# A hybrid Fourier and attention layer on one core: queues, engines and last rows changed, pl and the gate's sums in attention on GpSimd and ScalarE

## The chip, the cores and the metric

The kernel runs on one core of a Trainium2 chip. TensorE multiplies matrices into PSUM; VectorE (DVE), ScalarE (ACT) and GpSimd (POOL) work on tiles of 128 partitions; SyncE (SP) issues most DMAs, and ScalarE and GpSimd have DMA queues of their own. Each engine runs its own instructions in order. The metric is the device time of one execution in microseconds, as the median of several runs.

## The reference

One layer of a diffusion backbone over 1024 latent tokens (width 1024) with 256 context tokens, in float32. The cut below leaves out the rotary positions, the shapes and the context's own outputs.

```python
mod = silu(c) @ w_ada + b_ada
sh_m, sc_m, gt_m, sh_f, sc_f, gt_f = split(mod, 6)
h_lat = rms_norm(x, g_pre_mix) * (1 + sc_m) + sh_m
u_f, q_a, kv_a, kr = split(h_lat @ w_in)
q = rms_norm(q_a, g_q_a) @ w_q_b
k_nope, v = split(rms_norm(kv_a, g_kv_a) @ w_kv_b)
attn = softmax(q @ k.T * scale) @ v
four = fft2(u_f).real @ w_fourier
y = concat(four, attn) @ w_out
x = x + gt_m * rms_norm(y, g_post_mix)
h2 = rms_norm(x, g_pre_ffn) * (1 + sc_f) + sh_f
x = x + gt_f * rms_norm((silu(h2 @ w_gate) * (h2 @ w_up)) @ w_down, g_post_ffn)
```

There are 8 heads of 64 + 32 query columns, 1280 keys (latent and context), 4 Fourier groups of 128 channels, and 2816 hidden columns in the channel mixer.

## The kernel before, in words

**Products.** Every float32 product is made of three matmuls in a reduced format: a source is split into a high half, rounded by one engine (`split`, L50 on ScalarE), and a low half, the source minus the high half, made by VectorE (L56, written "v") or GpSimd (L58, written "p"). So each operand costs an operation on ScalarE and one on VectorE or GpSimd.

**Order.** The code is written as Python generators that interleave the work; a list scheduler turns it into one fixed instruction order for each engine and queue, starting from program order and from its own model of what is ready. Some instructions are pinned (`keep_in_program_order`), and `issue_after` puts a block behind one instruction of its engine. At run time each engine follows its order and waits on semaphores. A tile of a pool has `bufs` slots; a load into a slot waits until the slot's former readers are done.

**Stages.** (1) `constants` loads 83 rows of vectors, takes the Silu and transposes them. (2) `first_tiles` sweeps over j = 0 to 7: for each j it loads a block of w_ada (raw `araw`), splits it (ah, al), multiplies it with c (`modulation`: aps, then arow, cps, the shift SH and scale A), modulates a strip of x (h, L264), splits it (hh, hl), loads and splits a strip of w_in (`win_split`) and accumulates the projection of the first two token tiles. The modulation runs two steps ahead of the projection. `normed` (L198) loads a tile of x and normalises it. (3) `other_tiles` does the other eight token tiles, with `late_ada`, which sums w_ada's rows for two more modulations (`ada_sums`, L408), between them. (4) `fourier` does the DFT; in it `attention_weights` (L549) loads and splits the attention weights, and the keys, queries and maxima of head 0 are made. (5) `attention` (L584) goes over 8 heads and, in each, 10 blocks of 128 keys. For a block: scores S (6 matmuls), p32 = exp(S) on ScalarE, ph on ScalarE, pl on VectorE or GpSimd; two blocks later (LAG = 2) `pv` adds ph and pl times V into O. Between these steps `prepare` makes the next head's keys, queries (L686; the rotary part ends in the add of L701, then Qh on ScalarE and Ql on GpSimd) and `greatest` (L706), the maximum of each query's scores: 24 matmuls, each read by VectorE's reduction mx (L715). Their negatives become row 96 of Qh, by a DMA to DRAM from SP and one back from GpSimd. `finish` (L727) takes O and its sums through DRAM to get their reciprocals as rows, rb, and multiplies (L738). The gate gt_m is a sum of eight products of rows of w_ada with a column (`gate`, L441, `ada_sums`), one at blocks 3 and 8 of each head, by VectorE (L416, L418), behind its last split. (6) `output_weights` and `output_projection`. (7) `gate_up` and `down`, the channel mixer, with products cut down by Strassen-like sums; their operands are streamed through slots of `raw` and `unit`. (8) The end of `down`: the last products come in row tiles, the first halves of rows 0 to 3 (n = 2) and of rows 4 to 7 (n = 5), then the second halves of rows 0 to 3 (n = 3) and 4 to 7 (n = 4). For each row tile VectorE adds the bank to the accumulator (L1190), ScalarE takes the mean square, GpSimd the power -1/2 (L1212), VectorE scales by it and by the gate Gf (L1170), and GpSimd's DMA adds the row to `out` in DRAM. The last row tile is added to a copy of x1 loaded before, in two halves (L1175), and stored by SP and ScalarE.

Three spots of the code before:

```python
self.split(ph, pl, p32, "a", "v" if k % 3 == 1 or (h == HEADS - 1 and k % 2) else "p")
with tc.issue_after(self.lastv.ins):
    next(gate, None)
nc.sync.dma_start(self.max_d[h, :].rearrange("(b c) -> b c", b=NT), mrow)
nc.gpsimd.dma_start(Qh[96:97, :], self.max_d[h:h + 1, :])
```

Of the kernel before, what the change touches and what calls it, by code (L numbers as in the profile page):

```python
# [2 lines left out]

# [6 lines left out]
F32 = mybir.dt.float32  # L10
# [3 lines left out]
ALU = mybir.AluOpType  # L14
# [25 lines left out]
class Block:  # L40
# [49 lines left out]
    def build(self):  # L90
# [3 lines left out]
        with ExitStack() as top:  # L94
            self.cst = pool(top, "cst", side="left")
            self.dram = top.enter_context(tc.tile_pool(name="dram", bufs=1, space=DRAM))
            for name, n in (("xt", 7 * P), ("xtl", P), ("sum", HEADS), ("max", HEADS), ("inv", HEADS)):
                setattr(self, name + "_d", self.dram.tile([n, D], F32, name=name + "_d"))
# [68 lines left out]
    def constants(self):  # L167
        tc, nc, t, cst = self.tc, self.nc, self.t, self.cst
        rows = cst.tile([P, P], F32, name="rows")
        nc.sync.dma_start(rows[0:NROWS, :], t["rows"])  # L170
        self.ident = cst.tile([P, P], F32, name="ident")
        nc.sync.dma_start(self.ident, t["ident"])
        self.comb = cst.tile([4, 2], F32, name="comb")
        self.mhalf = cst.tile([P, 2], F32, name="mhalf")
        nc.vector.memset(self.mhalf, -0.5)
        self.ones = cst.tile([P, P], F32, name="ones")
        nc.vector.memset(self.ones, 1.0)
        nc.scalar.activation(rows[0:16, :], rows[0:16, :], AF.Silu)
        self.cols = cst.tile([P, NROWS], F32, name="cols")
        with tc.tile_pool(name="ps0", bufs=1, space=PSUM) as ps0:  # L180
            ps = ps0.tile([P, 512], F32, name="ps0")
            nc.tensor.transpose(ps[:, 0:NROWS], rows[0:NROWS, :], self.ident[0:NROWS, 0:NROWS])
            nc.vector.tensor_copy(self.cols, ps[:, 0:NROWS])
        cols = self.cols
        self.c4 = cst.tile([P, KT, 4], F32R, name="c4")
        cv = cols[:, 0:16].rearrange("p (a k) -> p k a", a=2)
        nc.vector.tensor_copy(self.c4[:, :, 0:2], cv)
        nc.vector.tensor_tensor(self.c4[:, :, 2:4], cv, self.c4[:, :, 0:2].bitcast(F32), ALU.subtract)
        self.b1 = cst.tile([P, 48], F32, name="b1")
        nc.vector.tensor_scalar(self.b1, cols[:, R_B:R_B + 48], 1.0, None, ALU.add)  # L190
        self.A = cst.tile([P, 2, KT], F32, name="A")
        self.SH = cst.tile([P, 2, KT], F32, name="SH")
        self.A2 = cst.tile([P, KT], F32, name="A2")
        self.SH2 = cst.tile([P, KT], F32, name="SH2")
        self.Gm = cst.tile([P, D], F32, name="Gm")


    def normed(self, src):  # L198

        nc = self.nc  # L200
        xs = self.xp.tile([P, D], F32, name="xs", bufs=2)
        nc.sync.dma_start(xs, src)
        r = self.rstd(self.xp, self.meansq(self.xp, xs, D))
        nc.gpsimd.tensor_scalar(xs, xs, r, 0.0, ALU.mult, ALU.add)
        return xs
# [12 lines left out]
    def first_tiles(self):  # L218
# [8 lines left out]
        def win_split(j):  # L227
            raw = sw.tile([P, 928], F32, name="wraw", bufs=3)
            nc.sync.dma_start(raw, t["w_in"][j * P:(j + 1) * P, :])
            wh, wl = (w[:, j, :] for w in self.win)  # L230
            self.split(wh, wl, raw, "a", "p")
            return wh, wl
        xT = sw.tile([P, KT, 2 * P], F32, name="xT")
        xs = [self.normed(t["x"][i * P:(i + 1) * P, :]) for i in range(2)]
# [14 lines left out]
        def modulation(j, ah, al):  # L249
# [6 lines left out]
            nc.vector.tensor_copy(row, ps[0:4, 0:256])  # L256
# [7 lines left out]
            nc.vector.tensor_scalar(h, xT[:, j, :], self.A[:, 0, j:j + 1], self.SH[:, 0, j:j + 1], ALU.mult, ALU.add)  # L264
# [143 lines left out]
    def ada_sums(self, part, acc, load):  # L408

        nc, t = self.nc, self.t  # L410
        for k in range(KT):
            raw = load()
            nc.sync.dma_start(raw, t["w_ada"][k * P:(k + 1) * P, part * D:(part + 1) * D])
            s = self.cols[:, R_C + k:R_C + k + 1]
            if k == 0:
                nc.vector.tensor_scalar(acc, raw, s, None, ALU.mult)  # L416
            else:
                nc.vector.scalar_tensor_tensor(acc, raw, s, acc, ALU.mult, ALU.add)  # L418
            yield
# [21 lines left out]
    def gate(self, part, G, g, load, bank):  # L441

        nc, t = self.nc, self.t
        yield from self.ada_sums(part, G, load)
# [13 lines left out]
        nc.vector.tensor_tensor(G, G, raw, ALU.mult)  # L458
# [16 lines left out]
    def fourier(self):  # L475
# [48 lines left out]
        self.split(wfh, wfl, wf, "a", "p")  # L524
        self.split(chh, chl, ch, "a", "p")
# [23 lines left out]
    def attention_weights(self):  # L549
# [20 lines left out]
        for k in range(2):  # L570
            w = [w[:, k, :] for w in self.wq]
            if k:
                weight(w, raws[k], R_GQ + k)
            else:
                nc.gpsimd.tensor_scalar(raws[k], raws[k], self.cols[:, R_GQ + k:R_GQ + k + 1], 0.0, ALU.mult, ALU.add)
                self.split(*w, raws[k], "a", "p")
            self.split(*(x[:, k, :] for x in self.qT), self.q32[:, k, :], "a", "v")
        yield
        self.split(*self.kvT, self.kv32, "a", "v")
        self.split(kh[64:96, :], kl[64:96, :], self.kr32[64:96, :], "a", "p")  # L580
# [3 lines left out]
    def attention(self, left):  # L584
        tc, nc, t, ap = self.tc, self.nc, self.t, self.ap
        with ExitStack() as es:
# [38 lines left out]
            gate = self.gate(2, self.Gm, t["g_post_mix"], lambda: self.early.tile([P, D], F32, name="adraw", tag="raw", bufs=1), self.bankW)  # L625
            for h in range(HEADS):
# [4 lines left out]
                def scores(k):  # L631
# [11 lines left out]
                    self.split(ph, pl, p32, "a", "v" if k % 3 == 1 or (h == HEADS - 1 and k % 2) else "p")  # L643
                    held.append((h, k, O, ph, pl))
                for k in range(NK):
                    if k in (3, 8):
                        with tc.issue_after(self.lastv.ins):
                            next(gate, None)
                    for _ in scores(k):
                        next(nxt, None)  # L650
                    if len(held) > LAG:
                        for _ in pv(*held.pop(0)):
                            next(nxt, None)
# [52 lines left out]
    def greatest(self, h, bank, pool):  # L706
# [14 lines left out]
        mrow = ap.tile([NT, P], F32, name="mrow", bufs=2)  # L721
        nc.vector.tensor_scalar(mrow, ps[0:NT, 0:P], -1.0, None, ALU.mult)
        nc.sync.dma_start(self.max_d[h, :].rearrange("(b c) -> b c", b=NT), mrow)
        nc.gpsimd.dma_start(Qh[96:97, :], self.max_d[h:h + 1, :])
        yield

    def finish(self, h, O):  # L727
# [10 lines left out]
        nc.vector.tensor_tensor(out[0:64, :], out[0:64, :], rb, ALU.mult)  # L738
# [164 lines left out]
    def all_loads(self):  # L903
# [9 lines left out]
        i = NT - 1  # L913
        yield self.raw(("x1", i), t["out"][i * P:(i + 1) * P, :])
# [195 lines left out]
    def down(self):  # L1110
# [50 lines left out]
        rows = [x[:, q].rearrange("p h c -> p (h c)") for x in (up, low) for q in range(4)]  # L1161
        pending = []

        def finish():

            while pending:
                i, r = pending.pop()
                where = t["out"][i * P:(i + 1) * P, :]
                if i + 1 < NT:
# [4 lines left out]
                for cs in (slice(0, 512), slice(512, D)):  # L1174
# [3 lines left out]
        for n, zh, wh in (2, 0, 0), (5, 1, 1), (3, 0, 1), (4, 1, 0):  # L1178
# [5 lines left out]
            for qs in ([0, 1], [2, 3]) if first else ([0], [1], [2], [3]):  # L1184
# [6 lines left out]
                for q in qs:  # L1191
# [3 lines left out]
                    final = i + 1 == NT  # L1195
                    v = f1.tile([P, 1], F32, name="var", bufs=16)
                    if first:
# [6 lines left out]
                        if final:  # L1204
                            pin(V(c, c, self.Gf[:, cs], ALU.mult))
                    else:
                        finish()
                        if final:
                            pin(V(c, c, self.Gf[:, cs], ALU.mult))
                        nc.scalar.activation(v, s, AF.Identity, bias=ss[i])  # L1210
                        r = f1.tile([P, 1], F32, name="rstd", bufs=4)
                        pin(nc.gpsimd.tensor_tensor(r, v, self.mhalf[:, 0:1], ALU.pow))  # L1212
                        pending.append((i, r))
# [67 lines left out]
```

## Time and profile before

| | us |
|---|---|
| median of 3 runs (1301.27 to 1303.33) | 1302.64 |
| the profiled execution | 1300.21 |
| its span in the trace | 1298.4 |
| TensorE busy in the span | 1222.3 (94%) |
| VectorE, ScalarE, GpSimd busy | 934.2, 633.5, 479.4 |
| mean granted clock of TensorE | 0.982 |

The profile covers one execution. An engine's busy time is the time in which an instruction of it runs; matmuls are pipelined, so a busy TensorE is not one at its peak. L50 is line 50 of the kernel; where a helper issues an operation (L50, L56, L58, L78) the tile's name tells which it is. "PE" is TensorE, "PEld" its weight load, an entry such as "[0.55 <-ACT hh L50]" an engine's idle time before an instruction and what ended it.

### The profile page before, as it was taken

Reading aid. Unit: us, or ns where it says so; the run is one execution under the profiler, and the core shown is the slowest. Engines: PE = TensorE matmul, PEld = TensorE weight load, DVE = VectorE, ACT = ScalarE, POOL = GpSimd, SP = SyncE. Lnnn points to the kernel's source line nnn. Section 1 sums busy time; section 2 is a strip of 40 time slices with the busy share of each in tenths; the row PEclk is TensorE's granted clock in tenths of the full one; section 3 lists DMA queues with packets and bytes.
Section 4 is the critical chain, followed back from the end, with each engine's and each line's share of the span. In section 5 each row is a group of like instructions: output and inputs, shape, how many; then the busy total and the mean of one; then the engine's idle time right before and its main releaser. Section 6 shows DMA issues by size and latency. Waiting matters only on the chain.

```text
span 1298.4 us, 15437 instructions
## 1 busy us (share of the span) xinstructions
PE 1222.3 (94%) x5474; PEld 955.1 (74%) x5474; DVE 934.2 (72%) x1301; ACT 633.5 (49%) x1045; POOL 479.4 (37%) x333
## 2 busy tenths in 40 slices
PE   5899978979999999889999999999999999999995
PEld 4588866756666666668788888888888887888884
DVE  6866586687675765353689887777777875898795
ACT  5467747646757668255644444433444433221232
POOL 4365556434555453253263332333311300000173
PEclk9999989989999999999999999999999999999998
DMA  8375211011110104642125554434454468987537
GB/s 318 127 246 169 69 49 36 31 33 46 38 33 17 34 18 139 179 140 101 60 81 179 178 178 149 150 110 144 163 178 154 153 212 335 344 296 256 194 130 130
DMA packets 79369, 181.64 MB, mean 140 GB/s; under 512 B 9569, under 2 KB 41332, under 8 KB 79292
## 3 DMA queue, kind: packets, MB, share of 16 engines
q1 hardware_dynamic: 67228, 137.89, 31.8%
q10 hardware_dynamic: 10800, 39.06, 7.7%
q0 software_dynamic: 1264, 3.70, 1.8%
q8 instruction: 43, 0.70, 0.2%
q14 instruction: 34, 0.28, 0.1%
HBM read 129.15 MB, written 51.48 MB: 139 GB/s over the span
## 4 chain that ended last, share of the span: by engine, by line
PE 49%; issue 2%; ACT 2%; POOL 2%; DVE 1%; DMA 1%; POOLq 0%; DVEq 0%; SPq 0%; ACTq 0%
PE gu L69 10%; PE gu L70 10%; PE gu L68 10%; PE y L774 5%; PE dn L68 4%; PE dn L70 4%; PE dn L69 4%; DMA unit<-zu 1%; DMA raw<-w_down 1%; POOL T L58 0%; POOL out_dram L1171 0%; PE T L209 0%; ACT H L321 0%; POOL rstd L1212 0%; DVE rows L1170 0%
## 5 line engine op out<-in xcount | busy, mean ns | idle before, releaser
L50 ACT ACTIVATE unit<-raw 128x512 fp32r<-128x512 f32 x171 | 105.5, 629 | 226.2 <-PE gu L70 106.3
L58 POOL TENSOR_TENSOR pl<-p,ph 128x1024 fp32r<-128x1024 f32 x53 | 128.8, 2431 | 148.0 <-ACT ph L50 111.6
L56 DVE TENSOR_TENSOR unit<-raw,unit 128x512 fp32r<-128x512 f32 x171 | 149.3, 881 | 27.3 <-ACT unit L50 26.9
L715 DVE TENSOR_REDUCE mx<-sps 128x1 f32<-128x512 f32 (+1 forms) x192 | 105.5, 594 | 31.5 <-PE sps L714 30.6
L640 ACT ACTIVATE p<-S 128x1024 f32<-128x1024 f32 x80 | 81.7, 1022 | 87.1 <-PE S L637 76.6
L935 POOL TENSOR_TENSOR s<-raw 128x512 f32<-128x512 f32 x22 | 33.8, 1537 | 241.4 <-DMA raw<-w_gate 167.9
L1155 POOL TENSOR_TENSOR rows<-rows,acc 128x512 f32<-128x512 f32 x8 | 13.5, 1705 | 212.8 <-DVE acc L1138 211.5
L50 ACT ACTIVATE ph<-p 128x1024 fp32r<-128x1024 f32 x80 | 84.3, 1057 | 1.9
L69 PE MATMUL gu<-T,unit 128*128 128x512 f32 x176 | 69.4, 394 | 0.9 <-POOL T L58 0.9
L70 PE MATMUL gu<-Bh,unit 128*128 128x512 f32 x176 | 69.4, 394 | 0.5 <-DVE unit L56 0.5
L68 PE MATMUL gu<-Bh,unit 128*128 128x512 f32 x176 | 69.4, 394 | 0.0
L69 PE MATMUL gu<-Bl,unit 128*128 128x512 f32 x176 | 69.3, 394 | 0.0
L70 PE MATMUL gu<-T,unit 128*128 128x512 f32 x176 | 69.3, 393 | 0.0
L68 PE MATMUL gu<-T,unit 128*128 128x512 f32 x176 | 69.2, 393 | 0.0
L68 PE MATMUL dn<-unit 128*128 128x512 f32 x148 | 58.2, 393 | 0.4 <-ACT unit L50 0.4
L70 PE MATMUL dn<-unit 128*128 128x512 f32 x148 | 58.0, 392 | 0.0
L69 PE MATMUL dn<-unit 128*128 128x512 f32 x148 | 58.0, 392 | 0.0
L621 PE MATMUL O<-pl,Vh 128*65 128x512 f32 x160 | 53.3, 403 | 4.6 <-POOL pl L58 3.8
L345 PE MATMUL acc<-win,hh 128*128 128x512 f32 (+1 forms) x224 | 55.8, 368 | 0.9 <-ACT hh L50 0.6
L1083 DVE TENSOR_TENSOR u<-u,gu 128x512 f32<-128x512 f32 x66 | 44.8, 681 | 15.6 <-PE gu L70 15.0
L78 POOL TENSOR_TENSOR rstd<-var,mhalf 128x1 f32<-128x1 f32 x44 | 27.6, 629 | 76.3 <-DVE var L76 75.6
L774 PE MATMUL y<-woh,xth 128*128 128x512 f32 x128 | 52.5, 410 | 2.4 <-ACT xth L50 2.4
(425 smaller groups left out, 3552.9 us busy)
## 6 DMA issues: line engine op xcount, KB each, us to landing
zu<-zpair ACTq DMA_DIRECT2D x50, 512.0 KB, 4.3
unit<-zu SPq DMA_DIRECT2D x47, 512.0 KB, 4.6
adraw<-w_ada SPq DMA_DIRECT2D x32, 512.0 KB, 3.9
units<-zu SPq DMA_DIRECT2D x27, 512.0 KB, 5.5
zu<-zone ACTq DMA_DIRECT2D x24, 512.0 KB, 3.1
raw<-w_gate SPq DMA_DIRECT2D x22, 512.0 KB, 4.2
raw<-w_up SPq DMA_DIRECT2D x22, 512.0 KB, 6.3
raw<-w_down SPq DMA_DIRECT2D x22, 512.0 KB, 5.2
```

The source lines that it names most:

```text
L50: nc.scalar.activation(hi, src, AF.Copy)
L56: self.lastv = nc.vector.tensor_tensor(lo, src, hi.bitcast(F32), ALU.subtract)
L58: nc.gpsimd.tensor_tensor(lo, src, hi.bitcast(F32), ALU.subtract)
L68: self.nc.tensor.matmul(out, ah, bh, start=i == 0, stop=False)
L69: self.nc.tensor.matmul(out, ah, bl, start=False, stop=False)
L70: self.nc.tensor.matmul(out, al, bh, start=False, stop=i == n - 1)
L345: nc.tensor.matmul(acc[:, o], a[:, k, :], b[:, k, c], start=k == 0 and n == 0, stop=k == KT - 1 and n == 2)
L621: nc.tensor.matmul(O[0:m, ns], a, b[:, ns], start=k == 0 and i == 0, stop=k == NK - 1 and i == 2)
L640: nc.scalar.activation(p32, S, AF.Exp, scale=SCALE)
L715: nc.vector.tensor_reduce(mx[:, i, c:c + 1], ps[:, 0:n], AX.X, ALU.max)
L774: nc.tensor.matmul(ps[:, ns], u[:, k, :], w[:, k, ns], start=k == 0 and i == 0, stop=k == KT - 1 and i == 2)
L1083: V(d, d, ps, ALU.add)
```

## The change

- The constants' 83 rows are padded to 96 for their load. The first two x tiles are loaded from ScalarE's queue.
- In the sweep, w_in's low half moves from GpSimd to VectorE, and the copy arow and the modulated strip h from VectorE to ScalarE.
- `ada_sums` issues each load one step ahead. With `apart`, ScalarE scales the row in place and GpSimd adds it.
- In `fourier` and `attention_weights` the low halves of w_fourier, the channel table, kr and the first half of wq move to VectorE, and that half of wq is scaled by ScalarE and VectorE.
- In attention GpSimd makes all pl of heads 0 to 6 and VectorE all of head 7. The gate is made `apart`, from two buffers, and without `issue_after`. The product with rb goes to GpSimd for heads 0 to 5. The maxima's row goes from mrow to Qh by one SP DMA; the DRAM tile `max` is gone.
- At the end, rows 4 to 7 are added to copies of x1 (four are loaded instead of one) and stored by SP; Gf is multiplied into another tile for them as soon as a half is summed; a row's finish stands behind the next row's power.

The diff, cut:

```diff
-        nc.sync.dma_start(rows[0:NROWS, :], t["rows"])
+        nc.sync.dma_start(rows[0:96, :], t["rows"])
...
-    def normed(self, src):
+    def normed(self, src, queue=None):
...
-        nc.sync.dma_start(xs, src)
+        (queue or nc.sync).dma_start(xs, src)
...
-            self.split(wh, wl, raw, "a", "p")
+            self.split(wh, wl, raw, "a", "v")
...
-        xs = [self.normed(t["x"][i * P:(i + 1) * P, :]) for i in range(2)]
+        xs = [self.normed(t["x"][i * P:(i + 1) * P, :], nc.scalar) for i in range(2)]
...
-            nc.vector.tensor_copy(row, ps[0:4, 0:256])
+            nc.scalar.activation(row, ps[0:4, 0:256], AF.Copy)
...
-            nc.vector.tensor_scalar(h, xT[:, j, :], self.A[:, 0, j:j + 1], self.SH[:, 0, j:j + 1], ALU.mult, ALU.add)
+            nc.scalar.activation(h, xT[:, j, :], AF.Identity, bias=self.SH[:, 0, j:j + 1], scale=self.A[:, 0, j:j + 1])
...
-    def ada_sums(self, part, acc, load):
+    def ada_sums(self, part, acc, load, apart=False):
...
-        for k in range(KT):
+        def fetch(k):
             raw = load()
             nc.sync.dma_start(raw, t["w_ada"][k * P:(k + 1) * P, part * D:(part + 1) * D])
+            return raw
+        raw = fetch(0)
+        for k in range(KT):
+            nxt = fetch(k + 1) if k + 1 < KT else None
             s = self.cols[:, R_C + k:R_C + k + 1]
-            if k == 0:
+            if apart:
+                nc.scalar.activation(raw if k else acc, raw, AF.Copy, scale=s)
+                if k:
+                    nc.gpsimd.tensor_tensor(acc, acc, raw, ALU.add)
+            elif k == 0:
                 nc.vector.tensor_scalar(acc, raw, s, None, ALU.mult)
...
+            raw = nxt
             yield
...
-        nc.vector.tensor_tensor(G, G, raw, ALU.mult)
+        (nc.gpsimd if apart else nc.vector).tensor_tensor(G, G, raw, ALU.mult)
...
-        self.split(wfh, wfl, wf, "a", "p")
-        self.split(chh, chl, ch, "a", "p")
+        self.split(wfh, wfl, wf, "a", "v")
+        self.split(chh, chl, ch, "a", "v")
...
-            w = [w[:, k, :] for w in self.wq]
-            if k:
-                weight(w, raws[k], R_GQ + k)
-            else:
-                nc.gpsimd.tensor_scalar(raws[k], raws[k], self.cols[:, R_GQ + k:R_GQ + k + 1], 0.0, ALU.mult, ALU.add)
-                self.split(*w, raws[k], "a", "p")
+            weight([w[:, k, :] for w in self.wq], raws[k], R_GQ + k)
...
-        self.split(kh[64:96, :], kl[64:96, :], self.kr32[64:96, :], "a", "p")
+        self.split(kh[64:96, :], kl[64:96, :], self.kr32[64:96, :], "a", "v")
...
+            rooms = cycle([(self.early, "raw"), (ap, "raw")])
+            def room():
+                pool, tag = next(rooms)
+                return pool.tile([P, D], F32, name="adraw", tag=tag, bufs=1)
+            gate = self.gate(2, self.Gm, t["g_post_mix"], room, self.bankW, apart=True)
...
-                    self.split(ph, pl, p32, "a", "v" if k % 3 == 1 or (h == HEADS - 1 and k % 2) else "p")
+                    self.split(ph, pl, p32, "a", "v" if h == HEADS - 1 else "p")
...
-                        with tc.issue_after(self.lastv.ins):
-                            next(gate, None)
+                        next(gate, None)
...
-        nc.sync.dma_start(self.max_d[h, :].rearrange("(b c) -> b c", b=NT), mrow)
-        nc.gpsimd.dma_start(Qh[96:97, :], self.max_d[h:h + 1, :])
+        nc.sync.dma_start(Qh[96:97, :].bitcast(F32).rearrange("o (b c) -> o b c", b=NT), mrow.bitcast(F32))
...
-        nc.vector.tensor_tensor(out[0:64, :], out[0:64, :], rb, ALU.mult)
+        (nc.vector if h >= HEADS - 2 else nc.gpsimd).tensor_tensor(out[0:64, :], out[0:64, :], rb, ALU.mult)
...
-        i = NT - 1
-        yield self.raw(("x1", i), t["out"][i * P:(i + 1) * P, :])
+        for i in range(NT // 2, NT):
+            yield self.raw(("x1", i), t["out"][i * P:(i + 1) * P, :])
...
-        rows = [x[:, q].rearrange("p h c -> p (h c)") for x in (up, low) for q in range(4)]
+        rows = [up[:, q].rearrange("p h c -> p (h c)") for q in range(4)]
+        rows += [a[n][:, q:q + 2].rearrange("p q c -> p (q c)") for n in (6, 1) for q in (0, 2)]
...
-                if i + 1 < NT:
+                if i < NT // 2:
...
-                for cs in (slice(0, 512), slice(512, D)):
+                for cs in [slice(0, 512), slice(512, D)] if i + 1 == NT else [slice(0, D)]:
...
-                    final = i + 1 == NT
+                    if zh:
+                        pin(V(rows[i][:, cs], c, self.Gf[:, cs], ALU.mult))
...
-                        if final:
-                            pin(V(c, c, self.Gf[:, cs], ALU.mult))
                     else:
-                        finish()
-                        if final:
-                            pin(V(c, c, self.Gf[:, cs], ALU.mult))
                         nc.scalar.activation(v, s, AF.Identity, bias=ss[i])
                         r = f1.tile([P, 1], F32, name="rstd", bufs=4)
                         pin(nc.gpsimd.tensor_tensor(r, v, self.mhalf[:, 0:1], ALU.pow))
+                        finish()
                         pending.append((i, r))
```

## Rows read from the trace of the kernel before

**Rows 1.** Stretches: us, busy PE, PEld, DVE, ACT, POOL (instructions), clock, DMA share, GB/s.
```profile
0.00:65.00 65.00, 45.41 (x264) 32.42 (x265) 46.79 (x68) 32.31 (x42) 24.79 (x19) 0.97 0.61 222
...
140.00:200.00 60.00, 49.30 (x256) 40.48 (x254) 43.15 (x74) 33.70 (x77) 32.54 (x38) 0.91 0.19 64
...
217.00:490.00 273.00, 258.87 (x1087) 177.25 (x1086) 193.91 (x284) 168.69 (x180) 134.64 (x62) 0.97 0.11 30
490.00:531.00 41.00, 34.31 (x137) 21.88 (x135) 24.32 (x16) 31.43 (x33) 13.83 (x6) 0.96 0.52 151
...
660.00:1268.00 608.00, 606.06 (x2637) 493.22 (x2636) 489.47 (x654) 222.81 (x384) 159.68 (x98) 1.00 0.54 191
1268.00:1298.40 30.40, 16.27 (x72) 13.03 (x70) 15.24 (x17) 7.75 (x24) 11.00 (x15) 0.85 0.81 139
```

**Rows 2.** Waits of TensorE: us in total, times, longest us.
```profile
PE sps L714 <- DVE mx L715: 10.8, 5, 6.6
...
PE qps L70 <- POOL wql L58: 4.3, 1, 4.3
...
PE O L621 <- POOL pl L58: 3.8, 4, 1.4
```

**Rows 3.** Timeline of VectorE, one sweep step: start, us, what, idle before.
```profile
48.56 1.22 DVE L56 TENSOR_TENSOR al<-araw,ah 128x1024 fp32r<-128x1024 f32 x1
...
49.89 3.17 DVE L56 TENSOR_TENSOR al<-araw,ah 128x1024 fp32r<-128x1024 f32 x1
52.98 0.40 DVE L264 TENSOR_SCALAR h<-xT,A,SH 128x256 f32<-128x256 f32 x1
...
54.21 0.40 DVE L256 COPY arow<-aps 4x256 f32<-4x256 f32 x1
...
55.51 1.22 DVE L56 TENSOR_TENSOR al<-araw,ah 128x1024 fp32r<-128x1024 f32 x1
```

**Rows 4.** Timeline of GpSimd in the same step.
```profile
49.79 2.19 POOL L58 TENSOR_TENSOR win<-wraw,win 128x928 fp32r<-128x928 f32 x1 [4.76 <-ACT win L50]
```

**Rows 5.** Timeline of ScalarE at the start.
```profile
4.80 0.31 ACT L178 ACTIVATE rows<-rows 16x128 f32<-16x128 f32 x1 [2.79 <-DMA rows<-rows]
6.22 1.06 ACT L86 ACTIVATE junk<-xs 128x1024 bf16<-128x1024 f32 x1 [1.11 <-DMA xs<-x]
```

**Rows 6.** Timeline of VectorE, weights of attention.
```profile
172.40 0.69 DVE L699 TENSOR_TENSOR tq<-qps,ropeq 32x512 f32<-32x512 f32 x1
```

**Rows 7.** Groups by form, 217 to 531 us.
```profile
L58 POOL TENSOR_TENSOR pl<-p,ph 128x1024 fp32r<-128x1024 f32 x53 | 128.8, 2431 | 148.0 <-ACT ph L50 111.6 <-PE S L637 22.4 <-issue 7.6
...
L418 DVE SCALAR_TENSOR_TENSOR Gm<-adraw,cols,Gm 128x1024 f32<-128x1024 f32 x7 | 17.5, 2503 | 0.0
L58 POOL TENSOR_TENSOR Ql<-q,Qh 96x1024 fp32r<-96x1024 f32 x7 | 17.4, 2481 | 15.5 <-ACT Qh L50 7.9 <-PE S L637 7.7
...
L701 DVE TENSOR_TENSOR q<-q,tq 32x512 f32<-32x512 f32 x14 | 13.8, 989 | 0.4
```

**Rows 8.** Timeline of VectorE, second head.
```profile
262.91 8.02 DVE L418 SCALAR_TENSOR_TENSOR Gm<-adraw,cols,Gm 128x1024 f32<-128x1024 f32 x1
```

**Rows 9.** Timeline of GpSimd, second head.
```profile
262.70 2.56 POOL L58 TENSOR_TENSOR Ql<-q,Qh 96x1024 fp32r<-96x1024 f32 x1 [2.09 <-ACT Qh L50]
265.22 4.63 POOL L58 TENSOR_TENSOR pl<-p,ph 128x1024 fp32r<-128x1024 f32 x2
```

**Rows 10.** Timeline of VectorE, last rows.
```profile
1286.20 0.68 DVE L1190 TENSOR_TENSOR rows<-rows,dn 128x512 f32<-128x512 f32 x1
1288.09 1.28 DVE L1170 SCALAR_TENSOR_TENSOR rows<-rows,rstd,Gf 128x1024 f32<-128x1024 f32 x1 [1.22 <-POOL rstd L1212]
...
1291.18 1.42 DVE L1175 SCALAR_TENSOR_TENSOR raw<-rows,rstd,raw 128x512 f32<-128x512 f32 x2 [1.21 <-POOL rstd L1212]
```

**Rows 11.** Timeline of GpSimd, last rows.
```profile
1287.18 0.87 POOL L1212 TENSOR_TENSOR rstd<-var,mhalf 128x1 f32<-128x1 f32 x1
...
1290.29 0.86 POOL L1212 TENSOR_TENSOR rstd<-var,mhalf 128x1 f32<-128x1 f32 x1
```

More of the change, by code (lines that the diff above doesn't have):

```diff
@@ L2 @@
 from contextlib import ExitStack
+from itertools import cycle
 import numpy as np
@@ L96, in build @@
             self.dram = top.enter_context(tc.tile_pool(name="dram", bufs=1, space=DRAM))
-            for name, n in (("xt", 7 * P), ("xtl", P), ("sum", HEADS), ("max", HEADS), ("inv", HEADS)):
+            for name, n in (("xt", 7 * P), ("xtl", P), ("sum", HEADS), ("inv", HEADS)):
                 setattr(self, name + "_d", self.dram.tile([n, D], F32, name=name + "_d"))
@@ L439, in ada_part, with gate @@
         yield
-    def gate(self, part, G, g, load, bank):
+    def gate(self, part, G, g, load, bank, apart=False):
         nc, t = self.nc, self.t
-        yield from self.ada_sums(part, G, load)
+        yield from self.ada_sums(part, G, load, apart)
         yield
@@ L624, in pv @@
                     self.finish(h, O)
-            gate = self.gate(2, self.Gm, t["g_post_mix"], lambda: self.early.tile([P, D], F32, name="adraw", tag="raw", bufs=1), self.bankW)
+            rooms = cycle([(self.early, "raw"), (ap, "raw")])
[3 more added lines that the diff above has]
+            gate = self.gate(2, self.Gm, t["g_post_mix"], room, self.bankW, apart=True)
             for h in range(HEADS):
@@ L720, in greatest @@
         nc.tensor.transpose(ps[0:NT, 0:P], m, self.ident)
-        mrow = ap.tile([NT, P], F32, name="mrow", bufs=2)
+        mrow = ap.tile([NT, P], F32R, name="mrow", bufs=2)
         nc.vector.tensor_scalar(mrow, ps[0:NT, 0:P], -1.0, None, ALU.mult)
-        nc.sync.dma_start(self.max_d[h, :].rearrange("(b c) -> b c", b=NT), mrow)
-        nc.gpsimd.dma_start(Qh[96:97, :], self.max_d[h:h + 1, :])
+        nc.sync.dma_start(Qh[96:97, :].bitcast(F32).rearrange("o (b c) -> o b c", b=NT), mrow.bitcast(F32))
         yield
@@ L1259 @@
     }
-    arrays["rows"] = np.concatenate([a[k].reshape(-1, P) for k in ("c", "c_ctx", "g_pre_mix", "g_pre_ffn", "b_ada", "g_q_a", "g_kv_a")])
+    rows = np.concatenate([a[k].reshape(-1, P) for k in ("c", "c_ctx", "g_pre_mix", "g_pre_ffn", "b_ada", "g_q_a", "g_kv_a")])
+    arrays["rows"] = np.concatenate([rows, np.zeros((96 - NROWS, P), rows.dtype)])
     arrays["w_ada_mix"] = arrays["w_ada"][:, :2 * D].reshape(KT, P, 2, KT, P).transpose(3, 1, 0, 2, 4)
```

## The prediction

> **What bounds the kernel now.** I read the stretches first, to see where TensorE is not busy [rows 1]. From 660 to 1268 us it works 606.06 of 608 us at full clock; nothing that the change does to other engines there can shorten it. The time to be had lies elsewhere: 19.6 us of 65 at the start, 10.7 of 60 around the weights of attention, 14.1 of 273 in the heads 0 to 6 (217 to 490 us), 6.7 of 41 in the last head, 14.1 of 30.4 at the end. The granted clock adds a little: a mean of 0.97 over the 273 us of the heads is a loss of about 8 us, of 0.91 over 60 us one of about 5; such a mean is made of short pieces at 1.2 GHz among 2.4.
>
> Then I read TensorE's waits for their causes [rows 2]: VectorE's maxima hold it 10.8 us, one wait of 6.6 among them; a low half made by GpSimd (wq, the query weights) 4.3; GpSimd's pl 3.8.
>
> The timelines name the mechanism behind the first. A sum of the gate on VectorE lasts 8.02 us [rows 8], its shape's mean is 2.50 [rows 7]. Meanwhile GpSimd runs Ql and two pl back to back, 262.70 to 269.85 [rows 9], and the sum ends 1.1 us behind them. So a VectorE operation with two SBUF operands stands still while GpSimd works, here through three operations, and the maxima queue behind it. The sweep at the start shows it again: of two equal al the first takes 1.22 us, the second, beside GpSimd's win of 2.19, takes 3.17 [rows 3, 4].
>
> **The sum, part by part.** The profiled execution took 1300.21 us (span 1298.4), 2.4 below the median 1302.64; the terms are taken from its rows and the 2.4 is added at the end. A measurement of this kernel tells 0.2%, about 2.6 us, from no change.
>
> *Start (0 to 65 us).* One sweep step lasts 6.95 us, from al at 48.56 to al at 55.51 [rows 3]. VectorE loses the blocked part of the second al (3.17 - 1.22 = 1.95), h (0.40) and arow (0.40), and gains win's low half, 1.22 x 928/1024 = 1.11. Net 1.64 a step. The eight passes of the sweep make seven steps, so 11.5 us at most: VectorE then wants 5.3 us a step, but TensorE works 45.41 of the 65 us [rows 1] and the chain arow, cps, A, h, hh, hl still changes engine five times. I take 60%, 7 us. The two x loads move past SP's queue to ScalarE's, where the Silu that waits for the rows' DMA ends at 5.11 and the first square takes x at 6.22 [rows 5]. In front of the Silu they go out at once, behind it they may cost 5 us. I take 0.5 of loss. ScalarE's new h and arow (0.4 each on VectorE now) fit: it is busy 32.31 of 65. Term: **-6.5**, between -11.5 and +5.
>
> *Weights (140 to 200 us).* TensorE's 4.3 us for wq's low half go: ScalarE and VectorE make it in place of GpSimd. But VectorE gets four low halves (kr 32x1280, wq, wf, ch), about 1.5 + 1.2 + 0.6 + 0.3 us by al's 1.22 for 1024 columns. These 3.6 us are about what the end of the blocking and of its own wait for wq's high half gives back to it. tq, from which the queries of head 0 follow, comes at 172.40 now [rows 6] and at about 172 then. What TensorE no longer waits for wq it waits for tq. Term: **-0.5**, between -4.3 and +2.
>
> *Heads 0 to 6.* Off VectorE: 21 pl (k = 1, 4, 7), the gate's seven sums, its first product and last one, six products with rb. Most of 10.8 us of waiting for maxima goes, and about half of the clock's 8 us, since the longest wait is what preceded the longest stretch at half clock: -14.8. On GpSimd, busy 134.64 of 273 us now, come 21 pl (2.43 each, 51.0), seven sums (17.0), one product (2.4), six products with rb (at Ql's 2.48, 14.9). Seven DMA issues go, uncounted. That makes 220 us, 31 a head, 86% of the 257 us that TensorE's term below would leave (273 - 16). ScalarE gets eight scalings of 1.06 (as the square of 1024 columns [rows 5]): 168.69 becomes 177 of 273. Two costs follow. L701, two in each head, is the one operation on VectorE with two SBUF operands left; it feeds Qh and so the next head's maxima. Today it takes 0.99 in the mean [rows 7]; unblocked an add of 512 columns takes 0.68 [rows 10]: 4.3 us lost in 14. With GpSimd busy 86 instead of 49% I take 1.75 times that, +3.2. And pl comes later: between S and its use lie exp, ph and pl, about 1.1 + 1.1 + 2.4 us (1024 columns each), against LAG = 2 steps; where a sum and a product with rb fall beside it GpSimd runs a backlog of 2.4 to 4.9 us. I take +4.6, the waits for pl in the kernel now and a fifth more. New waits: GpSimd waits for rb, ScalarE for w_ada rows, and pl and exp stand behind them; the rows are fetched a step ahead and land in time, rb is the open one. The maxima's row by one SP transfer, without GpSimd's, ends nothing: the row is due when the next head starts. Term: **-7**, between -22 (all the idle time and the clock) and +25 (rival below).
>
> The Trainium skill (SBUF — State Buffer, Who interferes with whom) states that a VectorE operation with two SBUF inputs contends with a GpSimd one that reads SBUF, that the later one is blocked for the whole instruction, and that a reduction never contends. By that rule L701 would wait for one GpSimd operation and no more, and the term would be about -10; rows 8 and 9 show a wait through three, and I keep the sum that goes by the rows.
>
> *Last head (490 to 531 us).* All ten pl go to VectorE, which is busy 24.32 of 41, and GpSimd falls silent. TensorE's waits for pl, 3.8 us [rows 2], I put here nearly whole: no other stretch of attention is idle for as large a share. ScalarE keeps its 31.43 us. Term: **-3**, between -6.7 and +1.
>
> *End.* Today each row goes round GpSimd: power 0.87, VectorE's L1170 1.28, the store's descriptors on GpSimd, then the next power behind them; the last rows come 3.1 us apart (powers at 1287.18 and 1290.29), slower than TensorE makes them: 72 matmuls in 16.27 us from 1268 [rows 1], so 12 for a row in 2.7. TensorE ends at 1284.27, but the last add starts at 1286.20 and the last product at 1291.18 [rows 10, 11]. In the change the power stands in front of the store, rows 4 to 7 need no GpSimd DMA, and Gf is multiplied into another tile without waiting. The last add then starts at 1284.3; add 0.68, Gf 0.68, row 6's product 1.28, and the last product starts at about 1287, 4.1 us earlier; four accumulating stores instead of seven give 0.4 more. Three loads of 512 KB more, at a DMA share of 0.54, and three SP stores stand beside TensorE's work. Term: **-4.5**, between -6.5 and -2.
>
> Sum: -6.5 - 0.5 - 7 - 3 - 4.5 = -21.5. 1300.2 - 21.5 = 1278.7; on the median's footing **1281 us**.
>
> **Rivals.** *GpSimd becomes the bound of the heads* (0.18). 31 us a head against 36.7 of TensorE, and some 34 in heads 1 to 3, with sums: backlogs eat the whole term, 1281 + 7 = 1288. For it: 86% in the mean; against it: heads without sums have a fifth of slack.
>
> The Trainium skill (GPSIMD Engine Reference, Engine selection) advises VectorE and not GpSimd for elementwise work, which is about twice as slow there; pl's 2.43 [rows 7] stands against al's 1.22 for as many columns [rows 3], so the trace agrees on the price. By that rule pl would have stayed, and this rival is what it fears.
>
> *All of it is released* (0.17): VectorE free of blocking lets TensorE go at its own pace: -11.5 - 0.5 - 18 - 4 - 5 = -39, 1264.
>
> *The start does not gain* (0.07): x behind the Silu, or the steps ordered by something else; 1281 + 6.5 = 1288. This is the change not doing what it says.
>
> *Slower: L701 starves* (0.08). It stands where GpSimd's backlog is largest, at the turn of heads. If it waits there through three operations, as L418 did, TensorE waits 6.6 us each time. The heads' term is then -14.8 + 6.6 n. The rest gives -14.5, so it decides from n = 5 on (-14.8 - 14.5 + 33 = +3.7); at all six turns it is +10.3, 1313.
>
> **How the numbers follow.** The forecast has 0.50, with 1274 to 1290 as its own range. 1262 to 1296 takes in all but the starving case and the ends of the others. Slower by over 0.2%: 0.08; within 0.2%: 0.04, the ends of the first and third rival; faster: 0.88.
>
> **What would show it.** Right: sweep steps of about 6 us without an al above 1.3; no L418 on VectorE; heads 0 to 6 shorter by 7 us with GpSimd at 80% or more; rows at the end 2.7 us apart, the last product within 3 us of TensorE's end. Wrong: L701 above 2 us in most heads, TensorE waiting for pl over 10 us in all, GpSimd idle in front of its product with rb, or a sweep step of still 6.9.

## The result and the profile after

The changed kernel takes 1286.84 us (median of 4 runs, 1284.62 to 1288.97) against 1301.95 for the kernel before (4 runs): a ratio of 0.9885, interval 0.9863 to 0.9907, or 15.1 us less. The profiled execution has a span of 1285.2 us, 13.2 less than 1298.4. The table sets the same instructions of both traces side by side: where each stage ends, and what each stage gained.

| end of stage | before | after | stage's change | predicted |
|---|---|---|---|---|
| last product of the projections | 153.2 | 146.4 | -6.8 | -6.5 |
| first scores of head 0 (weights, Fourier) | 210.2 | 207.7 | +4.4 | -0.5 |
| ScalarE copies O of head 6 | 497.3 | 491.2 | -3.7 | -7 |
| first product with w_out (last head) | 531.3 | 522.1 | -3.0 | -3 |
| last product of `down` | 1284.3 | 1276.6 | +1.4 | 0 |
| end of the span | 1298.4 | 1285.2 | -5.5 | -4.5 |

The first and the last parts did what was forecast, two stages in the middle did not. The stretches below lie about the second, third and fourth rows of the table; columns as in [rows 1].

```profile
140.00:200.00 60.00, 46.53 (x227) 37.18 (x227) 42.36 (x75) 32.55 (x70) 22.29 (x31) 0.86 0.28 91
...
217.00:490.00 273.00, 263.41 (x1107) 178.23 (x1107) 135.90 (x250) 179.06 (x190) 214.67 (x90) 0.99 0.11 30
490.00:531.00 41.00, 36.38 (x147) 23.06 (x146) 23.27 (x22) 27.48 (x30) 0.00 (x0) 1.00 0.59 175
```

Against [rows 1], VectorE in the heads falls from 193.91 to 135.90 and GpSimd rises from 134.64 to 214.67 (220 were forecast); TensorE is busy 4.5 us more there, and 2.8 less around the weights, where its clock falls from 0.91 to 0.86.

TensorE's waits of the whole kernel, as in [rows 2]; the waits for maxima are gone from the list, the wait for pl has doubled:

```profile
PE O L626 <- POOL pl L59: 7.8, 7, 2.7
...
PE Sp L71 <- DVE map1l L57: 3.7, 1, 3.7
...
PE mps L69 <- DVE zl L57: 2.5, 1, 2.5
...
PE po L69 <- ACT S L506: 2.1, 1, 2.1
...
PE dn L69 <- ACT unit L51: 1.6, 1, 1.6
```

**Head 0.** The whole wait for pl, all 7.8 us, lies here. GpSimd's timeline, from its Ql on:

```profile
223.98 2.41 POOL L59 TENSOR_TENSOR Ql<-q,Qh 96x1024 fp32r<-96x1024 f32 x1
226.33 2.41 POOL L423 TENSOR_TENSOR Gm<-Gm,adraw 128x1024 f32<-128x1024 f32 x1
228.67 2.41 POOL L59 TENSOR_TENSOR pl<-p,ph 128x1024 fp32r<-128x1024 f32 x1
231.01 2.42 POOL L423 TENSOR_TENSOR Gm<-Gm,adraw 128x1024 f32<-128x1024 f32 x1
...
252.83 2.39 POOL L423 TENSOR_TENSOR Gm<-Gm,adraw 128x1024 f32<-128x1024 f32 x1
```

All seven L423, the gate's sums, stand between 226 and 255 us, mostly one between two pl. The code still asks for one at blocks 3 and 8 of each head, but without `issue_after` they stand where the scheduler put them. TensorE then runs out of work, and its granted clock falls; stretches, columns as above:

```profile
245.00:252.00 7.00, 3.22 (x12) 1.79 (x12) 0.00 (x0) 3.66 (x4) 6.30 (x4) 1.00 0.42 126
252.00:258.80 6.80, 5.86 (x14) 4.47 (x15) 1.38 (x2) 4.96 (x7) 6.80 (x4) 0.50 0.43 146
```

TensorE is busy 3.2 of 7 us and then runs 6.8 us at 1.2 of 2.4 GHz. From its first scores to ScalarE's copy of O head 0 takes 59.0 us, 49.5 before; heads 1 to 6 take 38.0, 37.8, 38.0, 37.7, 39.8 and 33.0 against 43.7, 43.4, 36.0, 42.2, 39.9 and 32.4.

**The Fourier stage.** The gate's steps on ScalarE moved up as well. Its timeline:

```profile
177.10 1.15 ACT L421 ACTIVATE Gm<-adraw,cols 128x1024 f32<-128x1024 f32 x1 [3.23 <-DMA adraw<-w_ada]
...
182.29 1.15 ACT L421 ACTIVATE adraw<-adraw,cols 128x1024 f32<-128x1024 f32 x1 [2.70 <-DMA adraw<-w_ada]
183.35 0.58 ACT L506 ACTIVATE S<-Sp 128x512 f32<-128x512 f32 x1
```

ScalarE stands 2.7 us before a row of w_ada, the copy of Sp waits behind it, and TensorE waits 2.1 for that copy.

**The sweep.** VectorE's win, one for each step; it shows the step's length:

```profile
28.10 1.11 DVE L57 TENSOR_TENSOR win<-wraw,win 128x928 fp32r<-128x928 f32 x1
...
32.59 1.12 DVE L57 TENSOR_TENSOR win<-wraw,win 128x928 fp32r<-128x928 f32 x1
...
37.53 1.11 DVE L57 TENSOR_TENSOR win<-wraw,win 128x928 fp32r<-128x928 f32 x1
...
42.79 1.11 DVE L57 TENSOR_TENSOR win<-wraw,win 128x928 fp32r<-128x928 f32 x1
```

These steps take 4.5 to 5.3 us, and no al lasts over 1.24 us. The step of [rows 3], 6.95 us, is one of the longer ones: from the first to the last cps, seven steps, the mean is 6.4 us before and 4.7 now. The last four cps, the sweep's last modulation products, before and after:

```profile
61.82 0.60 PE L259 MATMUL cps<-comb,arow 4*128 4x2 f32 x4
```

```profile
50.89 0.60 PE L260 MATMUL cps<-comb,arow 4*128 4x2 f32 x4
```

They end at 62.42 before and at 51.49 now, 10.9 us earlier. At the end of the projections 6.8 of these are left. ScalarE's timeline behind the sweep, and then SP's queue:

```profile
56.99 1.06 ACT L87 ACTIVATE junk<-xs 128x1024 bf16<-128x1024 f32 x1 [3.97 <-DMA xs<-x]
```

```profile
34.16 19.64 SPq L203 DMA_DIRECT2D xs<-x  x3
```

Three loads of x are issued from 34.16 to 53.80; the third waits for a slot that the third x tile leaves when it is transposed. ScalarE waits 4.0 us for it, with the next modulation behind.

**The end.** VectorE's last rows, as in [rows 10], and GpSimd's powers, as in [rows 11]:

```profile
1275.22 1.28 DVE L1184 SCALAR_TENSOR_TENSOR raw<-acc,rstd,raw 128x1024 f32<-128x1024 f32 x1
1276.61 0.69 DVE L1199 TENSOR_TENSOR rows<-rows,dn 128x512 f32<-128x512 f32 x1
...
1279.66 1.42 DVE L1184 SCALAR_TENSOR_TENSOR raw<-acc,rstd,raw 128x512 f32<-128x512 f32 x2 [0.44 <-POOL rstd L1217]
```

```profile
1275.86 1.04 POOL L1217 TENSOR_TENSOR rstd<-var,mhalf 128x1 f32<-128x1 f32 x1 [1.66 <-ACT var L1215]
1278.58 1.04 POOL L1217 TENSOR_TENSOR rstd<-var,mhalf 128x1 f32<-128x1 f32 x1 [1.67 <-ACT var L1215]
```

Powers are 2.72 us apart (3.1 before). The last add starts at TensorE's end, the last product 3.1 us behind it; before it was 6.9.

### The profile page after: what moved, and what is told of

Same layout as the page of the kernel before. It is cut to its first block, busy times and chain, and to the rows that moved or that the text cites. A ratio compares the mean times of both kernels' runs of the same rounds, so it can differ in the third digit from the quotient of the medians.

```text
span 1285.2 us, 15444 instructions
## 1 busy us (share of the span) xinstructions
PE 1224.0 (95%) x5474; PEld 953.9 (74%) x5474; DVE 866.7 (67%) x1271; ACT 647.4 (50%) x1069; POOL 518.1 (40%) x340
## 3 DMA queue, kind: packets, MB, share of 16 engines
q1 hardware_dynamic: 67832, 139.99, 32.8%
## 4 chain that ended last, share of the span: by engine, by line
PE 51%; DMA 1%; ACT 1%; DVE 1%; issue 1%; POOL 1%; POOLq 0%; DVEq 0%; SPq 0%; ACTq 0%
PE gu L70 10%; PE gu L71 10%; PE gu L69 10%; PE dn L69 5%; PE dn L71 5%; PE dn L70 5%; PE y L781 5%; DMA unit<-zu 1%; DMA raw<-w_down 0%; POOL T L59 0%; PE T L210 0%; ACT H L322 0%; ACT unit L51 0%; DVE T6l L57 0%; DVE T7l L57 0%
## 5 line engine op out<-in xcount | busy, mean ns | idle before, releaser
L59 POOL TENSOR_TENSOR pl<-p,ph 128x1024 fp32r<-128x1024 f32 x70 | 168.5, 2409 | 59.0 <-ACT ph L51 37.7
L1090 DVE TENSOR_TENSOR u<-u,gu 128x512 f32<-128x512 f32 x66 | 44.9, 682 | 16.0 <-PE gu L71 15.3
```

The costliest lines, as they stand in the source:

```text
L59: nc.gpsimd.tensor_tensor(lo, src, hi.bitcast(F32), ALU.subtract)
L1090: V(d, d, ps, ALU.add)
```

## The experiments

Ratios are to the kernel before, measured beside each run, with the interval in brackets; a ratio is turned into us on a footing of 1301.

**Each part alone.** Four kernels apply one group each of the diff's edits to the kernel before (cut):

```diff
 start_only:   -  self.split(wh, wl, raw, "a", "p")          +  ... "a", "v"   (and x queue, arow, h, rows)
 weights_only: -  self.split(wfh, wfl, wf, "a", "p")         +  ... "a", "v"   (and ch, kr, wq)
 attn_only:    -  "v" if k % 3 == 1 or ... else "p"          +  "v" if h == HEADS - 1 else "p"   (and gate, rb, maxima's row)
 end_only:     -  yield self.raw(("x1", i), ...)             +  for i in range(NT // 2, NT): ...   (and all of the last rows)
```

> The kernel before with the change's first part alone: the padded rows, the two x loads from ScalarE's queue, win's low half on VectorE, arow and h on ScalarE. Theory: the part is worth what the traces show at the end of the projections (152.98 to 146.15 us, 6.8) and nothing behind it takes it back: 5 to 7 us faster than the kernel before. Rival: the weights of attention, whose loads then start no earlier, swallow it: 0 to 3 us faster.

> The kernel before with the change's weights part alone: the low halves of w_fourier, the channel table, kr and the first half of wq on VectorE. Theory: the 4.8 us that the changed kernel lost between the first weights and the first product with V came from the gate's steps placed there (ScalarE waits for a row of w_ada, S behind it, then half clock), not from VectorE's longer row: within 2 us of the kernel before. Rival: VectorE, without a pause for 16 us, is the bound there: 2 to 5 us slower.

> The kernel before with the change's attention part alone: all pl of heads 0 to 6 on GpSimd, the gate apart and untied, the product with rb, the maxima's row, the loads a step ahead. Theory: the first and the last part together were worth 14.6 of the change's 15.0 us, so this part as it stands gives back in head 0 and in the Fourier stage what it wins in heads 1 to 7: within 3 us of the kernel before. Rival: it is worth the 7 to 10 us that were predicted for the heads, and the sum of the parts is more than the whole because they cover each other: 7 to 10 us faster.

> The kernel before with the last part alone: four copies of x1, rows 4 to 7 added to them and stored by SP, Gf multiplied ahead, the power in front of the finish. By the traces the time from TensorE's last product to the end fell from 14.6 to 9.0 us (5.5), and one operand that came late in the channel mixer cost 1.5: 3.5 to 5.5 us faster than the kernel before. Rival: the three loads of 512 KB take more than 1.5 in this order: 0 to 2 us faster.

Measured: start 0.9941 [0.9924, 0.9958], -7.7 us; weights 0.9999 [0.9987, 1.001], nothing; attention 0.9984 [0.9972, 0.9996], -2.1; end 0.9947 [0.993, 0.9963], -6.9. Start and end gained more than was expected, the other two what was expected. They add up to -16.8 against the change's -15.1, within the intervals. Weights, heads and last head, forecast at -10.5 together, come to -2; what is missing is missing in attention. Its trace repeats the changed kernel's: head 0 takes 59.0 us, heads 1 to 3 38.1, 37.8 and 38.0, and TensorE's waits are

```profile
PE O L631 <- POOL pl L59: 7.8, 7, 2.7
```

The weights' own VectorE row costs nothing, and the 4.4 us lost there in the changed kernel belong to the gate's steps: from the last product of the projections to the first scores it is 57.0 us in the kernel before, 56.9 in weights_only and 60.9 in attn_only, where ScalarE's first two scalings stand in this stage too. The start's group was not taken apart: which of its edits made the sweep's gain is open.

**spread.** The gate's steps are tied again, now on two engines:

```diff
-                        next(gate, None)
+                        with tc.issue_after(self.lasta.ins), tc.issue_after(self.lastp.ins):
+                            next(gate, None)
```

> The changed kernel with the gate's steps tied again behind the last high half (ScalarE) and the last low half (GpSimd) traced before them, so that two sums fall in each head instead of seven in the first. Theory 1 (bunching): head 0 of the changed kernel is slow because seven sums of 2.4 us stand between its pl on GpSimd; spread, TensorE's 7.8 us of waits for pl nearly vanish, the piece at half clock in that head too, and ScalarE no longer waits 2.7 us for a row of w_ada before it copies S in the Fourier stage: 8 to 11 us faster than the changed kernel, 1276 to 1279. Rival (load): GpSimd with all pl, the sums and rb is too full for any head; the waits move to heads 1 to 3 with the sums, and the time stays at 1285 to 1289.

0.9897 [0.9876, 0.9918], 1286.4 us: nothing gained. That is the rival's time, but not the rival's reason. The trace shows that theory 1 is right where it looked: the first scores come at 201.8 us (207.7), head 0 takes 48.1 (59.0), and its waits for pl fall from 7.8 to 2.1. Then heads 1 to 6 take 42.1, 39.7, 41.7, 39.0, 42.5 and 35.9, in all 16.5 us more than in the changed kernel. The waits there are mostly not for pl (2.2 of the 4.4 us below); the three for Qh stand in heads 1, 3 and 5:

```profile
PE sps L723 <- ACT Qh L51: 8.1, 3, 2.7
PE O L626 <- POOL pl L59: 4.4, 5, 1.8
```

Qh waits for the add of the rotary part (L701 of the kernel before, L710 here). VectorE and GpSimd at the turn of head 2:

```profile
283.50 2.36 DVE L710 TENSOR_TENSOR q<-q,tq 32x512 f32<-32x512 f32 x1
...
287.30 1.67 DVE L710 TENSOR_TENSOR q<-q,tq 32x512 f32<-32x512 f32 x1
```

```profile
280.56 4.76 POOL L59 TENSOR_TENSOR pl<-p,ph 128x1024 fp32r<-128x1024 f32 x2
286.06 2.37 POOL L59 TENSOR_TENSOR pl<-p,ph 128x1024 fp32r<-128x1024 f32 x1 [0.75 <-POOL pl L59]
```

Each add ends 0.54 us behind the pl that ran when it started (285.86 after 285.32, 288.97 after 288.43). An add free of this lasts 0.68. It happens at three of the six turns of heads 1 to 6, and each time the clock drops behind it, from 290.5, 372.4 and 454.3 us on. The first drop, columns as above:

```profile
290.50:293.90 3.40, 3.40 (x10) 2.52 (x9) 1.72 (x3) 2.44 (x3) 3.40 (x2) 0.50 0.00 1
```

**psum_spread.** The same with one operand of the add in PSUM:

```diff
-            nc.vector.tensor_tensor(tq[64:96, :], ps[96:128, :], self.ropeq[96:128, ns], ALU.mult)
             nc.vector.tensor_tensor(q32[64:96, ns], ps[64:96, :], self.ropeq[64:96, ns], ALU.mult)
-            nc.vector.tensor_tensor(q32[64:96, ns], q32[64:96, ns], tq[64:96, :], ALU.add)
+            nc.vector.tensor_tensor(ps[64:96, :], ps[96:128, :], self.ropeq[96:128, ns], ALU.mult)
+            nc.vector.tensor_tensor(q32[64:96, ns], ps[64:96, :], q32[64:96, ns], ALU.add)
```

> The kernel with the spread gate, and one thing more: the rotary product is written over the projection's own PSUM bank instead of into the tile tq, so that the add that makes the rotary part of the queries has one operand in PSUM and one in SBUF. Theory 4 (blocking at the turns): with the sums spread, this add (two SBUF operands) is caught behind GpSimd's pl at the turns of heads 2, 4 and 6 (6 of 16 last 1.1 to 2.9 us, 20.7 in all), TensorE waits for Qh 2.9 us at each and drops to half clock behind it; this took back what head 0 had gained. With a PSUM operand no add should last over 0.75 us, and those three waits go: 8 to 13 us under the spread gate's 1286.4, so 1273 to 1278. Rival (order): TensorE waits there because ScalarE's Qh stands late in its order, whatever the add does: within 3 us of 1286.

0.9767 [0.9749, 0.9786], 1271.2 us: 15 less than spread (17 by the ratios), more than expected. The rival falls. The group of the adds in the heads, the same turn, and GpSimd beside it:

```profile
L709 DVE TENSOR_TENSOR q<-qps,q 32x512 f32<-32x512 f32 x14 | 9.6, 686 | 0.3
```

```profile
285.35 0.69 DVE L709 TENSOR_TENSOR q<-qps,q 32x512 f32<-32x512 f32 x1
```

```profile
282.31 4.75 POOL L59 TENSOR_TENSOR pl<-p,ph 128x1024 fp32r<-128x1024 f32 x2
```

The add runs at 285.35 in the middle of two pl and takes 0.69 us; spread's 14 took 19.3 (mean 1.38). In the heads TensorE no longer waits for Qh, and the clock is 1.00 from 205 to 500 us. Heads 1 to 6 take 39.5, 39.1, 39.2, 37.5, 39.9 and 32.8, together 13.0 us less than in spread.

**The edit without spreading, and on the kernel before.**

> The changed kernel with the rotary product in PSUM and nothing else; the gate's seven sums stay bunched in head 0. Theory (two costs that cover each other): with the sums bunched in head 0 GpSimd is idle at the later turns and only one add of 16 is held up (2.4 us at 214.9), so the edit alone is worth 0 to 3 us: 1282 to 1287. Rival (the add is the whole story, spreading is worth nothing): as fast as with both, 1270 to 1275.

> The kernel before with the rotary product in PSUM and nothing else. Theory: the adds in the heads take 13.8 us there against 9.6 free ones; the one of 2.8 at 350.97 left TensorE idle for 2.0, the others less, and the clock stayed up: 1 to 3 us faster than the kernel before. Rival: VectorE is held up there by GpSimd anyway, in pl, the sums and the product with rb, and the maxima come no earlier: within 1 us of it.

psum_after: 0.9851 [0.9832, 0.9871], 4.4 us better than the change, just over what was expected, and the intervals overlap; head 0 still takes 57.7 us. Of the 5.6 us gained in the span only 1.3 lie in head 0, where the one held add was; 2.4 lie ahead of the first scores, where TensorE waits 0.8 us for S instead of 2.1. Against the change, spreading alone gains nothing (0.9897 against 0.9885), PSUM alone 4.4 us, both together 15.3. So the two costs cover each other: with the sums bunched, the later turns find GpSimd idle. psum_before: 0.9958 [0.9944, 0.9973], -5.5 us, about twice what was expected; its rival falls too.

**lows, earlyx and the sum of the edits.** lows turns three splits (wf, ch, kr) back to `"a", "p"`; earlyx moves two conditions of the sweep:

```diff
-            if j == 4:   (the third and fourth x tile: load, normalise)
+            if j == 2:
-            if j == KT - 2:   (the third: transpose)
+            if j == 4:
```

> The changed kernel with the low halves of w_fourier, the channel table and kr on GpSimd again; the half of wq stays on VectorE. Theory 2: between 154.6 and 170.2 us VectorE works without a pause, GpSimd is idle from 149.7 to 170.7, and TensorE waits for zl (2.5) and map1l (3.7) at the end of that row; 2.6 us of low halves less on VectorE let both come 2.6 earlier: 2.5 to 4 us faster, 1283 to 1284.5. Rival: GpSimd's operations hold up VectorE's with two SBUF operands as in the kernel before (wql 1.99, wvl 2.83), and nothing is gained: 1286 to 1288.

> The changed kernel with the third and fourth x tiles loaded and normalised two steps of the sweep earlier and the third transposed two steps earlier, so that the slot for the fifth is free sooner. Theory 3: of the 10.9 us that the sweep gained, 5.7 are given back behind it, because the fifth x tile is loaded only when the third has been transposed; ScalarE stands 4.0 us before its square, with the modulation of the third tile queued behind, and TensorE is idle from 58.1 to 61.6 and then at half clock to 67.7. Free the slot earlier and 3 to 5 us come back: 1282 to 1284. Rival: the next stage waits for something else as well (rows of w_ada, slots of the hh tiles), and TensorE's work to the end of the projections is what it is: within 1 us of 1287.

> All three edits together. If theories 1 to 3 hold and their places are apart (0 to 70, 150 to 190, 215 to 260 us), the gains add up: 13 to 20 us faster than the changed kernel, 1267 to 1274. If the weights' wait only passes what was won before it on to the next wait, about 10: 1277.

> The same edit on top of all three edits. Theory 4: the waits of 2.9 us at the turns of heads 2 and 4 go, and the clock's drop of 6.8 us behind the first: 5 to 8 us under 1281.7, so 1274 to 1277. Rival (order): 1280 to 1283.

lows: 0.9883 [0.9861, 0.9904], no difference, as its rival said. 2.6 us leave VectorE, and another operation with two SBUF operands is caught behind kr's K0l; VectorE and GpSimd:

```profile
159.48 3.07 DVE L578 SCALAR_TENSOR_TENSOR wvl<-wkraw,cols,wvh 128x512 fp32r<-128x512 f32 x1 [0.25 <-ACT wvh L577]
```

```profile
158.78 3.23 POOL L59 TENSOR_TENSOR K0l<-kr32T,K0h 32x1280 fp32r<-32x1280 f32 x1 [8.31 <-PE kps L71]
```

(0.75 us for wvl in the changed kernel.) earlyx: 0.9861 [0.9837, 0.9884], 3.1 us better than the change, the low end of what was expected. The intervals overlap, so the traces decide: the last product of the projections ends at 142.7 us here (146.4 in the changed kernel) and at 141.7 and 141.8 in all3 and psum_all3, but at 145.2 to 147.6 in the other runs that have the start's edits. The load of the fifth x tile, which ended SP's group of three at 53.80, is issued at 43.36 in earlyx:

```profile
43.36 0.33 SPq L203 DMA_DIRECT2D xs<-x  x1
```

all3: 0.986 [0.9836, 0.9883], 1281.7 us, short of the 1267 to 1277 expected: earlyx's gain alone, with the turns of heads 2 and 4 as in spread. psum_all3: 0.9744 [0.9723, 0.9765], 1267.58 us, 33 under the kernel before and 18 under the change, the lowest median of all (its interval overlaps that of psum_spread). It is 14 us under all3, where 5 to 8 were expected.

## Why the prediction was right, and where it was wrong

Range and sign held: 1286.84 lies in 1262 to 1296 and in the forecast's own 1274 to 1290. The size was over-told: 21.5 forecast, 15.1 measured, 13.2 in the spans of the two traces. The 8.3 us missing there are 4.9 in the stage of the weights, 3.3 in heads 0 to 6 and 1.4 in `down`, less 1.3 that start and end gained beyond their terms. The first two have one cause, the gate's untied steps.

**Start**, -6.5: -6.8 in the trace, -7.7 alone. Steps fell by 1.7 us in the mean, all of the 1.64 and not 60% of it, and 4.1 of the 10.9 us went back behind the sweep. That seam had no term, so that the sum comes out within 0.3 us is luck; earlyx, whose third to fifth x tiles come earlier, wins 3.7 of it back in the trace. The price read from [rows 3] holds for the sweep before: behind each of the last seven win on GpSimd one operation of VectorE stood still for 1.4 to 2.0 us, four times al, twice h and once hl. The x loads did go out ahead of the Silu (ScalarE issues them from 0.73 us), so the 5 us bound to them was not needed.

**Weights**, -0.5, up to +2: alone nothing, as forecast; in the change +4.4, outside its bounds. The step that failed stands in the heads' part: "the rows are fetched a step ahead and land in time". They do not: the gate's scalings were placed in the Fourier stage, ScalarE waited 2.7 us for one with S behind it, and spread, which moves them away, won 4.7 us there (61.4 against 56.7 us from the projections' end to the first scores, with the clock's drops in both).

**Heads 0 to 6**, -7: -3.7 in the trace. The released waits are there (heads 1 to 6 are 13.1 us shorter, against -14.8 for all seven), but head 0 costs 9.4. That the two costs of the forecast, 7.8 together, come near this is luck: L701's did not occur, and the longer wait for pl, 7.8 us against 3.8 in the whole kernel, came in one head, with a drop of the clock behind it. The sums were counted, 17 us of GpSimd over seven heads, and not asked where they would stand once `issue_after` was gone. A mean of 86% says nothing where 17 of 17 us fall into one head. For L701 +3.2 was put in; the adds took 0.81 us in the mean against 0.99 [rows 7]. "It stands where GpSimd's backlog is largest, at the turn of heads" was wrong for the changed kernel, whose GpSimd idles there. The starving rival's mechanism is real, though, in a weaker form: in spread an add stood behind one pl, not three operations, at three turns, at 4.3 us each with the clock (13.0 for three). With 3.4 more for the sums in their new heads this took the 15.6 us that spreading had won in head 0 and ahead of it. Its condition was another order of the work.

**Last head**, -3: -3.0; 3.6 of the 3.8 us of waits for pl did lie there. **End**, -4.5: -5.5. `down`, which had no term, is 1.4 us longer, with a wait of 1.6 for an operand (unit). The x1 loads, named beside TensorE's work and priced at nothing, are not shown to cost this: attn_only, which loads one x1 tile as the kernel before does, has the same wait,

```profile
PE dn L69 <- ACT unit L51: 1.6, 1, 1.6
```

and end_only, with the four loads, has none for a split, but one of 1.5 for a load (`zu`). From the first product with w_out to the last of `down` the runs spread from 750.7 to 756.0 us (753.0 in the kernel before), so what made the 1.4 stays open.

Of the rivals, "GpSimd becomes the bound of the heads" came nearest in time (1288), for a bound in head 0 alone. "All of it is released" (1264) did not come, but the runs show what it needed: with both costs removed it is 1271.2, and 1267.6 with the x tiles earlier as well.

By the sentence of the Trainium skill cited in the prediction (SBUF — State Buffer, Who interferes with whom) an add waits for one GpSimd operation. The adds here agree: every one that was caught ends about half a microsecond behind the operation that ran. But GpSimd paused behind each of those, so they do not test a row of operations without a pause, as in [rows 9]. In the kernel before, a low half on VectorE does (VectorE, then GpSimd):

```profile
80.02 1.77 DVE L56 TENSOR_TENSOR hl<-h,hh 128x512 fp32r<-128x512 f32 x1
```

```profile
78.99 3.94 POOL L58 TENSOR_TENSOR tol<-traw,toh 128x512 fp32r<-128x512 f32 x2
```

It ends at 81.79, in the middle of GpSimd's second operation. So the wait of L418 through three [rows 8] was not the rule; why it came to that is open. Heads 1 to 3 of psum_spread are still 1.1 to 1.5 us longer than in the changed kernel, with the sums that now stand there; this was not taken apart further.

## What to carry to other kernels

When a tie that held work in its place is taken away, ask where the scheduler will put the work, and sum the load by stretch, not over the stage. Where GpSimd is busy throughout, give VectorE's short sums and products on the path one operand in PSUM; here a product written over its own PSUM bank did that without a further instruction. An experiment that gains nothing may have gained and lost the same: compare stage by stage before a theory is dropped.

## What the hardware showed that was not expected

An add of 512 columns with both operands in SBUF took up to 2.90 us beside a pl on GpSimd, with one of them in PSUM 0.68 to 0.69 in every one of 16. The Trainium skill (SBUF — State Buffer, Who interferes with whom) states that an instruction of VectorE with at most one SBUF input, outside VectorE's 2-port modes, does not contend with GpSimd. The adds agree, and here they decided 15 us with the sums spread and 5.5 in the kernel before.

One SBUF operand was not enough everywhere. In the kernel before, h, with one tile and two scalars for each partition as inputs, was caught behind GpSimd's win:

```profile
37.10 2.12 DVE L264 TENSOR_SCALAR h<-xT,A,SH 128x256 f32<-128x256 f32 x1
```

```profile
36.89 2.18 POOL L58 TENSOR_TENSOR win<-wraw,win 128x928 fp32r<-128x928 f32 x1 [4.70 <-ACT win L50]
```

It ends 0.15 us behind win; free it takes 0.40 [rows 3]. Whether h ran in one of those 2-port modes, no run here shows.
